# Left factors of the output and FFN projections: turned blocks kept in SBUF, their sums and splits placed by written lists

## The chip, the cores and the metric

One Trainium2 chip, one core. The metric is the device time of one execution in microseconds (us); lower is better. The kernel before takes 1965.07 us, the median of 3 runs (1964.33 to 1965.67). Traces come from one execution each, taken by the hardware profiler.

## What is computed

One layer of a decoder, for 512 tokens (S) of width 2048 (D), all in float32. Cut to what matters here:

```python
h    = rms_norm(x, norm1_g)
proj = h @ w_in                                    # 512 x 2048 @ 2048 x 6160
qa, ka, va, ra, ga, qb, kb, vb = split(proj)
out_a = rms_norm(gated_linear_attention(qa, ka, va, gate(ga))) * silu(ra)   # 4 heads, 512 x 1024
out_b = dilated_attention(norm(qb), norm(kb), vb)                           # 8 heads, 512 x 1024
x  = x + concat(out_a, out_b) @ w_out              # 512 x 2048 @ 2048 x 2048
h2 = rms_norm(x, norm2_g)
x  = x + (silu(h2 @ w_gate) * (h2 @ w_up)) @ w_down   # hidden width 5632
```

## The kernel before

**Products.** Each large matrix product is cut in 2 x 2 blocks and done with seven block products in place of eight (Strassen's way). The left factor of each of the seven is a block of the activations or a sum of blocks; its names are A11, S1, S2, S4, S3, A12 and A22, in the order in which `PRODUCTS` uses them (P1, P5, P6, P3, P7, P2, P4). The right factor is a block of the weights or a difference of blocks. To keep float32 accuracy, each factor is split in a rounded high part and a low remainder, both fp32r, and TensorE multiplies high by high, low by high and high by low: 12 matmuls of 128x512.

**Pairs and items.** A `Pair` (L236) computes 1024 output columns. It is a chain of *items*: seven products times the operand's *groups* (4 as a rule, each 256 + 256 rows of the contraction), so 28 items of 12 matmuls, 336 in all (L358). `stream` (L318) runs all pairs back to back. For item k it emits the high part of the weights of item k+1 (ACT, L331), the difference of weight blocks for item k+2 where the product needs one (DVE, L256; P5, P6, P7 and P4 do), the low part of item k+1 (DVE, L335), then the matmuls of item k. The high and the low weight tiles have two buffers each, so these two engines can be about one item ahead of TensorE.

**The order of the pairs.** Input projection: va, qb0/kb0, vb, qb1/kb1, and the *gate pair* (the columns ra). Output projection: *out0* and *out1*. Then eleven FFN pairs (*ffn0* to *ffn10*), then six down-projection pairs. The left factors of the output projection are held by `opm`, those of the FFN by `opn`.

**Making a left factor.** `Operand.split` (L161, L162) makes one of seven factors of one group: a cast on ACT and a subtraction on DVE, each 128x512. The four sums S1 to S4 take four more DVE operations of that size for each group. So one group costs 11 DVE operations of 128x512, 7 of them the remainders of splits. I call each of these 11 a *unit*.

**Results of a pair.** When a product's last item is done, `later` closes the result some items later: the two row halves of each 512-column half come out after items 15 (P3), 19 (P7), 23 (P2) and, in the next pair, after its item 0 (P4). In the gate pair `final_gate` (L1037) multiplies them by the mixed output of the first heads; in out0 and out1 `final_out` (L1201) adds the residual. Two items after that, `transposed_store` (L1012) turns the 256x512 piece with 8 TensorE transposes (L1019), copies the two 128x512 blocks out of PSUM on ACT (L1027, L1030) and stores each of them in DRAM (L1034): `mix_d` for the gate pair and the dilated heads, `xn_d` for out0 and out1. All DMAs of this part are issued by one queue, SP.

**Background work.** What a later pair needs runs as generators in the list `background`. After the high matmuls of each item `step` (L519) fires what `later` has put off and then takes as many units of the first generator as the pair's pace says. In the gate pair these are the last four dilated heads (`dil_heads(4)`, `dil_heads(6)`), and from `early_job` and `late_jobs` (L1078, L1112) the factors of `opm`: every block is loaded from DRAM again, each time that it is used (`top`, and the tiles r, v, T, qT, kT), 8 loads for each group. `early` (L205) loads two blocks, splits A11, forms S3 (L215) and splits it; `late_jobs` forms S1 (L1121), S2 (L1123), S4 (L1125) with a split each, and splits A12 and A22. Before out0 begins, `finish` (L535) forces `early` to its end, whatever the pace says. For `opn`, groups 0 and 1 are made by `operand_jobs` (L1155, `build` L178) during out1, and groups 2 and 3 by `early_job` and `late_jobs` at the end of out1 and in ffn0, again with `finish` before ffn0.

The order on an engine isn't quite the order in the text: the builder moves an instruction ahead where its inputs are ready, so the text sets priorities and not a fixed sequence. Waits are then met in the order of the engine's queue.

Of the kernel before, what the change touches and what calls it, by code (L numbers as in the profile page):

```python
# [10 lines left out]
F32 = mybir.dt.float32  # L11
# [3 lines left out]
ALU = mybir.AluOpType  # L15
# [3 lines left out]
P = 128  # L19
# [4 lines left out]
DK = 128  # L24
DV = 256
NB = 640
PRODUCTS = ("P1", "P5", "P6", "P3", "P7", "P2", "P4")
UPPER_FIRST = ("P1", "P2", "P5", "P6", "P3", "P7", "P4")

# [67 lines left out]
def block_kernel(ctx: ExitStack, tc: tile.TileContext, ins, out):  # L97
# [19 lines left out]
    def nm(s):  # L117
        uid[0] += 1
        return f"{s}_{uid[0]}"
# [846 lines left out]
    def in_turn(*gens):  # L966
        for g in gens:
            yield from g


    def heads_norm(t):
# [4 lines left out]
        for h in range(4):  # L976
# [35 lines left out]
    def transposed_store(tiles, half, dsts, gains=None, spare=None):  # L1012

        for b in range(2):
            bk = bank().rearrange("p (j n) -> p j n", j=2)
            for jj in range(2):
                for m in range(2):
                    f = (2 * b + jj) * P
                    nc.tensor.transpose(  # L1019
                        bk[:, jj, m * P : (m + 1) * P], tiles[m][:, f : f + P], ident  # L1020
                    )
            if spare is None:
                d = work(("oT", "PT")[b], (P, 2, 256))
            else:
                d = spare[:, b]
            if gains is None:
                nc.scalar.copy(d, bk)  # L1027
            else:
                for jj in range(2):
                    nc.scalar.activation(  # L1030
                        d[:, jj, :], bk[:, jj, :], AF.Copy,
                        scale=gains[:, 2 * b + jj : 2 * b + jj + 1],
                    )
            store(dsts[b][half], d)  # L1034
            done.add((id(dsts[b]), half))

    def final_gate(half, which, tiles, acc_):  # L1037
# [11 lines left out]
        for m in range(2):  # L1049
# [10 lines left out]
            nc.scalar.activation(tiles[m], tiles[m], AF.Ln, bias=1.0)  # L1060
            nc.scalar.activation(tiles[m], tiles[m], AF.Exp, scale=-1.0)
            nc.vector.tensor_tensor(tiles[m], tiles[m], og[m], op=ALU.mult)
        spare = apool.tile([P, 2, 2, 256], F32, name=nm("turned"), tag="A")
        later(2, lambda: transposed_store(
            tiles, half, mix_d[2 * which : 2 * which + 2], spare=spare
        ))

    def part(src, half):
        def get(t=None):
# [4 lines left out]
            return t  # L1074

        return get

    def early_job(op, wanted, flip):  # L1078
        h0, h1 = (1, 0) if flip else (0, 1)
        return op.early([(g, part(top, h0), part(top, h1)) for g, top in wanted])  # L1080

    def staged(items, ahead=1):

# [25 lines left out]

        return (id(src), half), fetch  # L1110

    def late_jobs(op, groups, tops, bots, flip):  # L1112

        h0, h1 = (1, 0) if flip else (0, 1)
        tt = nc.vector.tensor_tensor
        sums = {}

        def sum_of(name, g, op1):
            def use(t):
                if name == "S1":  # L1120
                    tt(sums[g], t, sums[g], op=ALU.add)  # L1121
                elif name == "S2":
                    tt(sums[g], sums[g], t, op=ALU.subtract)  # L1123
                else:
                    tt(sums[g], t, sums[g], op=ALU.subtract)  # L1125
                op.split(name, g, sums[g])

            return use

        def both(g):  # L1130
            fetch = fetch_part(tops[g], h1)[1]

            def get():
                sums[g] = part(bots[g], h1)()
                return fetch()

            return (id(bots[g]), h1), get

        items = []
        for part_ in groups:  # L1140
            for g in part_:
                items.append((*both(g), sum_of("S1", g, op)))
            for g in part_:
                items.append((*fetch_part(tops[g], h0), sum_of("S2", g, op)))
        groups = [g for part_ in groups for g in part_]
        for g in groups:
            items.append((*fetch_part(bots[g], h0), sum_of("S4", g, op)))
        for name, half in (("A12", h0), ("A22", h1)):
            for g in groups:
                items.append(  # L1150
                    (*fetch_part(bots[g], half), lambda t, name=name, g=g: op.split(name, g, t))
                )
        return staged(items)

    def operand_jobs(op, tops, bots, lo, hi):  # L1155
        def job():
# [30 lines left out]
    def residual(tiles, acc_, rows, c0, src):  # L1187
# [10 lines left out]
                res.append(tiles[m])  # L1198
        return res

    def final_out(second):  # L1201
        def final(half, which, tiles, acc_):
            tok = 1 - half
            rows = [2 * tok, 2 * tok + 1]
            ch = 2 * second + which
            tiles = residual(
                tiles, acc_, rows, 512 * ch, lambda t, c: x[t * P : (t + 1) * P, c : c + 512]
            )
            for m in range(2):
                t = rows[m]  # L1210
                store(x1_d[t][:, 512 * ch : 512 * ch + 512], tiles[m])
                jk = work("L", bufs=2)
                nc.scalar.activation(
                    jk, tiles[m], AF.Square, accum_out=ss2[:, t, ch : ch + 1]
                )
            dsts, gains = xn_d[2 * ch : 2 * ch + 2], g2[:, 4 * ch : 4 * ch + 4]

            def turn():
                transposed_store(tiles, tok, dsts, gains)
                if not second and which == 0 and half == 1:  # L1220
                    background.append(operand_jobs(opn, tops, bots, 0, 2))
                elif second and which == 1 and half == 1:
                    background.append(early_job(opn, [(g, tops[g]) for g in (2, 3)], False))
                    background.append(late_jobs(opn, ((2, 3),), tops, bots, False))

            later(3 if which == 0 and half == 1 else 2, turn)
            if second and which == 0 and half == 1:
                for n in range(3):
                    later(1 + n, lambda n=n: output_scales(n))

        return final

    ocol = lambda c: w_out[:, c // 512]
    def output_scales(part):
# [6 lines left out]
        else:  # L1241
# [190 lines left out]
```

## Time and profile before

| | |
|---|---|
| median of 3 runs | 1965.07 us |
| profiled execution | 1958.01 us, span 1956.1 us |
| TensorE's granted clock, mean | 0.999 |
| ACT busy | 1088.1 us, 56% of the span |
| DMA moved | 362.52 MB, 185 GB/s |
| HBM read, written | 298.68 MB, 64.51 MB |

The span runs from the first to the last instruction in the trace; the profiled execution lasted 1.9 us longer than it. In the profile PE is TensorE's matmuls, PEld its weight loads, DVE VectorE, ACT ScalarE, SP the queue that issues the DMAs; L358 is line 358 of the kernel. A window's row gives its length, and for each engine the busy time and, after an x, the number of instructions. A row of a timeline gives start, duration, engine, line, what is written from what, and in brackets how long the engine was idle before it and what ended that. Records of a few matmuls can be missing or stand in a neighbouring window.

### The profile page before, as it was taken

How to read it: one execution, taken by the hardware profiler on the slowest of the kernel's cores; microseconds unless marked ns; L12 is line 12 of the kernel's file. 1: busy time of each engine (PE TensorE's matmuls, PEld its weight loads, DVE VectorE, ACT ScalarE, POOL GpSimd, SP SyncE). 2: the span in 40 equal slices, each digit the busy share in tenths (PEclk: the TensorE clock that was granted, in tenths of full speed). 3: DMA queues.
4: the chain of work that ended last, by engine and by line, in shares of the span. 5: the costliest groups of instructions: out<-in, count | busy, mean ns of one | idle time of the engine just before them, and what ended most of it. 6: DMA issues, size and time to landing. Idle time of an engine off the chain costs nothing.

```text
span 1956.1 us, 25599 instructions
## 1 busy us (share of the span) xinstructions
PE 1918.2 (98%) x9160; PEld 1657.3 (85%) x9160; DVE 1648.0 (84%) x1845; ACT 1088.1 (56%) x1580; POOL 55.2 (3%) x73
## 2 busy tenths in 40 slices
PE   8999999999999999999999999999999999999998
PEld 6788888888878888888888888888888888888887
DVE  7996887768789989878878879879879989989977
ACT  9654554667666665544544545545546646546443
POOL 0000330011000000000000000000000000000000
PEclk9999999999999999999999999999999999999999
DMA  9545555444567584453453453443445865855662
GB/s 355 174 154 206 179 173 171 143 156 162 198 217 241 181 289 148 154 188 141 155 183 135 162 182 120 171 171 124 173 170 176 279 212 182 292 198 180 230 215 76
DMA packets 158855, 362.52 MB, mean 185 GB/s; under 512 B 16438, under 2 KB 43359, under 8 KB 158728
## 3 DMA queue, kind: packets, MB, share of 16 engines
q1 hardware_dynamic: 158584, 360.89, 53.1%
q8 instruction: 71, 1.16, 0.2%
q14 instruction: 56, 0.46, 0.1%
q10 hardware_dynamic: 144, 0.01, 0.0%
HBM read 298.68 MB, written 64.51 MB: 186 GB/s over the span
## 4 chain that ended last, share of the span: by engine, by line
PE 75%; DVE 6%; DMA 3%; issue 2%; ACT 1%; SPq 0%; POOL 0%; DVEq 0%; ACTq 0%
PE acc L358 71%; DVE wl L335 2%; PE bank L1019 1%; DVE wa L256 1%; PE bank L926 1%; PE bank L904 1%; DVE AS L162 1%; PE bank L919 0%; DMA xn_d<-PT 0%; DMA q<-y_d 0%; PE bank L895 0%; DMA q<-in_x 0%; DMA T<-p_d 0%; DMA r<-xn_d 0%; ACT wh L331 0%
## 5 line engine op out<-in xcount | busy, mean ns | idle before, releaser
L358 PE MATMUL acc<-wh,AS 128*128 128x512 f32 x3008 | 712.2, 379 | 0.9 <-DVE AS L162 0.8
L358 PEld LDWEIGHTS acc<-wh,AS 128*128 128x128 f32 x3008 | 568.0, 189 | 82.8 <-DVE AS L162 1.6
L331 ACT CAST wh<-wa 128x1024 fp32r<-128x1024 f32 x376 | 394.3, 1049 | 395.1 <-PE acc L358 365.2
L358 PE MATMUL acc<-wh,AA 128*128 128x512 f32 x2256 | 533.7, 379 | 1.1 <-ACT wh L331 0.9
L335 DVE TENSOR_TENSOR wl<-wa,wh 128x1024 fp32r<-128x1024 f32 x376 | 458.7, 1223 | 74.5 <-ACT wh L331 45.6
L358 PEld LDWEIGHTS acc<-wh,AA 128*128 128x128 f32 x2256 | 426.0, 189 | 62.7 <-ACT wh L331 2.3
L358 PE MATMUL acc<-wl,AS 128*128 128x512 f32 x1504 | 395.3, 385 | 7.6 <-DVE wl L335 7.5
L358 PEld LDWEIGHTS acc<-wl,AS 128*128 128x128 f32 x1504 | 279.2, 189 | 61.0 <-DVE wl L335 20.3
L358 PE MATMUL acc<-wl,AA 128*128 128x512 f32 x1128 | 296.1, 385 | 3.4 <-DVE wl L335 3.3
L358 PEld LDWEIGHTS acc<-wl,AA 128*128 128x128 f32 x1128 | 209.3, 189 | 35.8 <-DVE wl L335 7.5
L331 ACT CAST wh<-wb 128x1024 fp32r<-128x1024 f32 x94 | 98.6, 1049 | 123.8 <-PE acc L358 117.1
L331 ACT CAST wh<-wc 128x1024 fp32r<-128x1024 f32 x94 | 98.4, 1047 | 109.2 <-PE acc L358 106.6
L331 ACT CAST wh<-wd 128x1024 fp32r<-128x1024 f32 x94 | 98.6, 1049 | 103.6 <-PE acc L358 98.5
L335 DVE TENSOR_TENSOR wl<-wc,wh 128x1024 fp32r<-128x1024 f32 x94 | 115.0, 1223 | 41.7 <-ACT wh L331 41.7
L335 DVE TENSOR_TENSOR wl<-wd,wh 128x1024 fp32r<-128x1024 f32 x94 | 114.8, 1223 | 37.8 <-ACT wh L331 28.7
L256 DVE TENSOR_TENSOR wa<-wc,wa 128x1024 f32<-128x1024 f32 x94 | 114.8, 1225 | 35.6 <-DMA wc<-in_w_gate 20.8
L335 DVE TENSOR_TENSOR wl<-wb,wh 128x1024 fp32r<-128x1024 f32 x94 | 114.5, 1221 | 5.3 <-ACT wh L331 4.9
L256 DVE TENSOR_TENSOR wa<-wb,wa 128x1024 f32<-128x1024 f32 x94 | 113.8, 1222 | 1.7 <-DMA wb<-in_w_in 1.0
L256 DVE TENSOR_TENSOR wb<-wd,wb 128x1024 f32<-128x1024 f32 x94 | 114.8, 1223 | 0.4
L256 DVE TENSOR_TENSOR wa<-wd,wa 128x1024 f32<-128x1024 f32 x94 | 113.5, 1223 | 0.1
L298 DVE SCALAR_TENSOR_TENSOR seed<-acc,rs,seed 128x512 f32<-128x512 f32 x96 | 70.5, 747 | 27.6 <-PE acc L358 27.5
L282 ACT ACTIVATE seed<-acc,rs 128x512 f32<-128x512 f32 x96 | 60.8, 682 | 3.1 <-PE acc L358 3.1
(285 smaller groups left out, 1332.2 us busy)
## 6 DMA issues: line engine op xcount, KB each, us to landing
wa<-in_w_gate SPq DMA_DIRECT2D x44, 512.0 KB, 3.4
wb<-in_w_up SPq DMA_DIRECT2D x44, 512.0 KB, 4.0
wd<-in_w_up SPq DMA_DIRECT2D x44, 512.0 KB, 4.1
wc<-in_w_gate SPq DMA_DIRECT2D x44, 512.0 KB, 3.4
wc<-in_w_in SPq DMA_DIRECT2D x28, 512.0 KB, 3.5
wa<-in_w_in SPq DMA_DIRECT2D x24, 512.0 KB, 4.9
wb<-in_w_in SPq DMA_DIRECT2D x24, 512.0 KB, 5.7
wd<-in_w_in SPq DMA_DIRECT2D x24, 512.0 KB, 5.1
```

The source lines that it names most:

```text
L162: nc.vector.tensor_tensor(a[:, :, 1, :], src, a[:, :, 0, :].bitcast(F32), op=ALU.subtract)
L256: nc.vector.tensor_tensor(src, self.quarter(one, g), src, op=ALU.subtract)
L282: nc.scalar.activation(halves(t), unfolded(src[m]), AF.Copy, scale=self.scale(half, m))
L298: nc.vector.scalar_tensor_tensor(halves(seed[m]), unfolded(src[m]), self.scale(half, m), halves(seed[m]), op0=ALU.mult, op1=ALU.add,)
L331: nc.scalar.copy(high[k], sources[k])
L335: nc.vector.tensor_tensor(low[k], sources.pop(k), high[k].bitcast(F32), op=ALU.subtract)
L358: nc.tensor.matmul(p.dst[prod][m], a[:, jj, hl, m * P : (m + 1) * P], folded(w[:, jj, :]), start=fresh and g == 0 and len(terms) == 2 and ...
L904: nc.tensor.matmul(lp[:, :n], qh[:, b * P : (b + 1) * P], kh[:, :n], start=True, stop=True)
L926: nc.tensor.matmul(op, vh[:, k, :], lgs[b][:, k * P : (k + 1) * P], start=(k == 0), stop=(k == b))
L1019: nc.tensor.transpose(bk[:, jj, m * P : (m + 1) * P], tiles[m][:, f : f + P], ident)
```

## The change

The text of the four pairs around the output projection is changed in three ways.

1. **The gate pair's turned blocks stay in SBUF.** `transposed_store` gets no destination there, so the 8 stores to `mix_d` are gone; the blocks lie in tiles of `apool` or in the work tiles qT, kT, v, T, and are found in `kept`. The blocks of the dilated heads still go through DRAM, and each is now loaded once (`T`), kept, and used for A11, S3, S2 and S1. S2 is formed before S1, in place: S2 = r1 - S3, then S1 = S2 + A11.
2. **The same for the second half of `opn`**: out1's turned blocks stay in work tiles ("t") and in `rpool` ("r"), and `kept_job` makes groups 2 and 3 in the order of `KEPT`, without a load or a store.
3. **Where the units stand.** In the gate pair and in out0 a written list says after which item's step each unit is emitted; `early_job`, `late_jobs` and the forced `finish` before out0 are gone. The `finish` before ffn0 now asks for A11 of group 3 only. The paces of ffn0 change, and out0's last result is turned one item earlier.

```diff
+KEPT = "A11.2 A11.3 =S3.2+S3.2 =S3.3+S3.3 =S2.2+=S1.2+S1.2 =S2.3+=S1.3+S1.3 S2.2 S2.3 =S4.2+S4.2 =S4.3+S4.3 A12.2 A12.3 A22.2 A22.3"
+GATE = {
+    9: "T.0 T.1",  11: "A11.0",  12: "S3.0",  13: "A11.1",  14: "S3.1",  16: "T.2",
+    18: "A11.2",  19: "S3.2",  21: "2.0 S1.0",  22: "2.1",  23: "S1.1",  24: "S2.0",
+    25: "T.3 S2.1",  27: "A11.3",
+}
+OUT = {
+    0: "S3.3",  2: "2.2 S1.2",  3: "2.3 S1.3",  4: "S2.2",  5: "S2.3",  9: "S4.0",
+    10: "S4.1",  11: "S4.2",  12: "S4.3",  17: "A12.0 A12.1",  18: "A12.2",  19: "A12.3",
+    21: "A22.0",  22: "A22.1",  24: "A22.2",  25: "A22.3",
+}
...
         "qb1": lambda: [
             dil_heads(4),
-            together(dil_heads(6), in_turn(*(early_job(opm, [(g, mix_d[4 + g])], True) for g in range(3)))),
-            early_job(opm, [(3, mix_d[7])], True),
-            late_jobs(opm, ((0, 1), (2, 3)), mix_d[4:], [mix_d[b] for b in order], True),
+            dil_heads(6),
         ],
...
+            if dsts is None:
+                continue
             store(dsts[b][half], d)
...
-        spare = apool.tile([P, 2, 2, 256], F32, name=nm("turned"), tag="A")
-        later(2, lambda: transposed_store(
-            tiles, half, mix_d[2 * which : 2 * which + 2], spare=spare
-        ))
+        def turn():
+            if which == 1:
+                t = apool.tile([P, 2, 2, 256], F32, name=nm("turned"), tag="A")
+                spare = [t[:, 0], t[:, 1]]
+            else:
+                spare = [work(n, (P, 2, 256)) for n in (("qT", "kT"), ("v", "T"))[half]]
+            transposed_store(tiles, half, None, spare=spare)
+            for b in range(2):
+                kept[2 * (which == 0) + b, "r" + str(1 - half)] = spare[b]
+        later(2, turn)
...
+        if name == "T":
+            t = apool.tile([P, 2, 2, 256], F32, name=nm("top"), tag="A")
+            for i in range(2):
+                kept[g, "t" + str(i)] = part(mix_d[4 + g], 1 - i)(t[:, i])
+            return
+        t0, t1 = kept[g, "t0"], kept[g, "t1"]
+        if name == "A11":
+            opm.split(name, g, t0)
+        elif name == "S3":
+            tt(t1, t0, t1, op=ALU.subtract)
+            opm.split(name, g, t1)
+        elif name == "2":
+            tt(t1, kept[g, "r1"], t1, op=ALU.subtract)
+            tt(t0, t1, t0, op=ALU.add)
+        elif name == "S1":
+            opm.split(name, g, t0)
+        elif name == "S2":
+            opm.split(name, g, t1)
+        elif name == "S4":
+            tt(t1, kept[g, "r0"], t1, op=ALU.subtract)
+            opm.split(name, g, t1)
+        else:
+            opm.split(name, g, kept[g, "r0" if name == "A12" else "r1"])
...
-    pair(opx, rows_in, col(2048), col(2560), final_gate, rate((27, 0.72), (1, 0)), row_scale)
+    pair(opx, rows_in, col(2048), col(2560), final_gate, scripted(rate((27, 0.72), (1, 0)), GATE), row_scale)
...
             def turn():
-                transposed_store(tiles, tok, dsts, gains)
-                if not second and which == 0 and half == 1:
-                    background.append(operand_jobs(opn, tops, bots, 0, 2))
-                elif second and which == 1 and half == 1:
-                    background.append(early_job(opn, [(g, tops[g]) for g in (2, 3)], False))
-                    background.append(late_jobs(opn, ((2, 3),), tops, bots, False))
-
-            later(3 if which == 0 and half == 1 else 2, turn)
+                if not second:
+                    transposed_store(tiles, tok, dsts, gains)
+                    if which == 0 and half == 1:
+                        background.append(operand_jobs(opn, tops, bots, 0, 2))
+                        background.append(kept_job(opn, kept_n))
+                    return
+                if which == 1:
+                    kept_n["t", tok] = [work(n, (P, 2, 256)) for n in (("qT", "kT"), ("v", "T"))[tok]]
+                else:
+                    kept_n["r", tok] = [
+                        rpool.tile([P, 2, 256], F32, name=nm("r"), tag="r") for _ in range(2)
+                    ]
+                transposed_store(tiles, tok, None, gains, spare=kept_n["tr"[which == 0], tok])
+
+            later(2, turn)
...
-    pair(opm, rows_mix, ocol(0), ocol(512), final_out(0), paced([1] * 28),
-         before=lambda: finish(lambda: ("S3", 3) in opm.t))
+    pair(opm, rows_mix, ocol(0), ocol(512), final_out(0), scripted(step, OUT))
...
-    paces = {0: [0, 1, 1, 1, 1, 0, 0, 1, 1] + [0] * 6, 10: [0] * 6}
+    paces = {0: [1, 1, 1, 1, 0, 0, 0, 0, 0, 0, 1, 1, 1, 1, 0, 0, 0, 0], 10: [0] * 6}
     def before_ffn(j):
         if j == 0:
-            finish(lambda: ("S3", 3) in opn.t)
+            finish(lambda: ("A11", 3) in opn.t)
```

The lists are shortened here to fewer lines. `scripted` (not shown) calls the pair's pace and then emits the words that the list has for the item. `kept_job` (not shown) goes through `KEPT`, one word for each step; it waits, without emitting anything, until the blocks that a word needs are there; a word with "=" forms the sum, one without it is the split.

More of the change, by code (lines that the diff above doesn't have):

```diff
@@ L1110, in fetch_part @@
         return (id(src), half), fetch
-    def late_jobs(op, groups, tops, bots, flip):
-        h0, h1 = (1, 0) if flip else (0, 1)
-        tt = nc.vector.tensor_tensor
[L1116 to L1153, printed above, removed]
@@ L1199, in residual, with kept_job @@
         return res
+    kept_n = {}
+    def kept_job(op, kept):
+        tt = nc.vector.tensor_tensor
+        sums = {
+            "S3": ("t1", "t0", "t1", ALU.subtract), "S2": ("t1", "r1", "t1", ALU.subtract),
+            "S1": ("t0", "t1", "t0", ALU.add), "S4": ("t1", "r0", "t1", ALU.subtract),
+        }
+        parts = {"A11": "t0", "S3": "t1", "S1": "t0", "S2": "t1", "A12": "r0", "S4": "t1", "A22": "r1"}
+        have = lambda n: (n[0], int(n[1])) in kept
+        for word in KEPT.split():
+            for one in word.split("+"):
+                name, *g = one.split(".")
+                split = name in parts and one[0] != "="
+                name = name.strip("=")
+                g = int(g[0])
+                needs = [parts[name]] if split else sums[name][:3]
+                while not all(have(n) for n in needs):
+                    yield
+                at = lambda n: kept[n[0], int(n[1])][g - 2]
+                if split:
+                    op.split(name, g, at(parts[name]))
+                else:
+                    d, a, b, how = sums[name]
+                    tt(at(d), at(a), at(b), op=how)
+            yield
     def final_out(second):
```

47 lines of the change are left out of this document (43 added, 4 removed).

## Prediction

> **What bounds the kernel now.** I read the page first.
>
> ```profile
> span 1956.1 us, 25599 instructions
> PE 1918.2 (98%) x9160; PEld 1657.3 (85%) x9160; DVE 1648.0 (84%) x1845; ACT 1088.1 (56%) x1580; POOL 55.2 (3%) x73
> q1 hardware_dynamic: 158584, 360.89, 53.1%
> ```
>
> TensorE bounds the whole, with VectorE close behind as an average. So I looked for stages in which TensorE runs below its pace: windows of the item line alone, cut so that each holds one pair of 336 matmuls (gate pair, out0, out1, ffn0, ffn1), then the same windows for the transposes (L1019; out0, out1, ffn0, ffn1), and from the chain the price of eight transposes.
>
> ```profile
> 453.37:558.54 105.17, 78.64 (x338) 62.45 (x336) 1.00 0.54 187
> 558.54:642.12 83.58, 76.09 (x338) 62.41 (x336) 1.00 0.64 214
> 642.12:720.81 78.69, 75.32 (x337) 62.21 (x336) 1.00 0.64 219
> 720.81:801.98 81.17, 74.49 (x336) 62.97 (x337) 1.00 0.57 193
> 801.98:876.27 74.29, 73.03 (x337) 63.20 (x336) 1.00 0.45 160
> ```
>
> ```profile
> 558.54:642.12 83.58, 5.25 (x38) 4.29 (x38) 1.00 0.64 214
> 642.12:720.81 78.69, 4.15 (x32) 3.75 (x32) 1.00 0.64 219
> 720.81:801.98 81.17, 2.08 (x16) 1.87 (x16) 1.00 0.57 193
> 801.98:876.27 74.29, 2.07 (x16) 1.87 (x16) 1.00 0.45 160
> ```
>
> ```profile
> 809.05 0.87 PE bank L1019 x8
> ```
>
> ffn1 is the undisturbed pair: 74.29 us, with 16 transposes at 0.87/8 = 0.109. Without them (1.74) 336 matmuls take 72.55, so 0.216 each and 2.59 for an item. Above that pair, and with 0.109 for every further transpose taken off, out0 loses 83.58 - 74.29 - 22 x 0.109 = **6.9 us**, out1 78.69 - 74.29 - 16 x 0.109 = **2.7**, ffn0 81.17 - 74.29 = **6.9**. The gate pair carries the dilated heads' matmuls too, so there I take only the visible idle time of PE, from windows of all engines (columns: PE, PEld, DVE, ACT, POOL, clock, DMA share, GB/s):
>
> ```profile
> 453.37:500.00 46.63, 44.76 (x237) 37.44 (x236) 38.22 (x63) 32.34 (x74) 4.88 (x4) 1.00 0.34 111
> 500.00:544.40 44.40, 43.98 (x241) 38.19 (x240) 35.07 (x63) 32.10 (x65) 0.00 (x0) 1.00 0.64 224
> 544.40:558.54 14.14, 13.04 (x65) 10.86 (x63) 9.90 (x14) 9.31 (x14) 0.00 (x0) 1.00 0.91 322
> 558.54:597.99 39.45, 35.09 (x159) 27.69 (x158) 39.42 (x48) 26.46 (x39) 0.00 (x0) 1.00 0.38 127
> 597.99:642.12 44.13, 44.13 (x219) 38.81 (x217) 42.61 (x49) 30.27 (x51) 0.00 (x0) 1.00 0.87 292
> 698.00:720.81 22.81, 22.70 (x113) 19.53 (x112) 16.46 (x19) 13.18 (x25) 0.00 (x0) 1.00 0.96 325
> 720.81:759.66 38.85, 33.43 (x152) 27.67 (x153) 36.56 (x46) 26.59 (x44) 0.00 (x0) 1.00 0.52 174
> 801.98:876.27 74.29, 74.29 (x353) 65.01 (x352) 60.28 (x59) 37.15 (x43) 0.00 (x0) 1.00 0.45 160
> ```
>
> That is 1.87 + 0.42 + 1.10 = **3.4 us**. So everything within reach of this change is 6.9 + 2.7 + 6.9 + 3.4 = 19.9 us, about 1% of the span. The rows also say where it lies: all of out0's loss is in its first 12 items (from 597.99 on PE is busy without a gap), and there DVE is busy 39.42 of 39.45 us. All of ffn0's loss is in its first 12 items too (12 x 2.59 + 0.87 = 32.0 of 38.85), with DVE at 36.56. Just ahead of both, DVE stood still: 4.2 us in 544.40 to 558.54, 6.4 in 698 to 720.81.
>
> The clearest view is the ledger of loads. PEld is busy 65.01/74.29 = 87.5% in the undisturbed pair, 70% in out0's first 12 items and 71% in ffn0's. [...]
>
> What DVE did, and what PE waited for, from their timelines:
>
> ```profile
> 465.65 0.68 DVE L162 TENSOR_TENSOR AA<-top,AA 128x512 fp32r<-128x512 f32 x1
> ...
> 548.31 0.69 DVE L1121 TENSOR_TENSOR r<-v,r 128x512 f32<-128x512 f32 x1 [3.91 <-DMA v<-mix_d]
> ...
> 556.05 0.69 DVE L215 TENSOR_TENSOR top<-top 128x512 f32<-128x512 f32 x1
> ...
> 560.55 1.22 DVE L335 TENSOR_TENSOR wl<-wa,wh 128x1024 fp32r<-128x1024 f32 x1
> ...
> 562.82 0.69 DVE L162 TENSOR_TENSOR AA<-top,AA 128x512 fp32r<-128x512 f32 x1
> 563.42 0.69 DVE L162 TENSOR_TENSOR AS<-top,AS 128x512 fp32r<-128x512 f32 x1
> 564.03 0.69 DVE L162 TENSOR_TENSOR AS<-r,AS 128x512 fp32r<-128x512 f32 x1
> ...
> 596.81 0.68 DVE L1125 TENSOR_TENSOR r<-qT,r 128x512 f32<-128x512 f32 x1
> ...
> 619.62 0.69 DVE L162 TENSOR_TENSOR AA<-kT,AA 128x512 fp32r<-128x512 f32 x1
> ```
>
> ```profile
> 719.25 0.69 DVE L215 TENSOR_TENSOR top<-top 128x512 f32<-128x512 f32 x1 [3.08 <-DMA top<-xn_d]
> 719.86 0.69 DVE L162 TENSOR_TENSOR AA<-top,AA 128x512 fp32r<-128x512 f32 x1
> 722.42 0.69 DVE L215 TENSOR_TENSOR top<-top 128x512 f32<-128x512 f32 x1 [1.87 <-DMA top<-xn_d]
> ...
> 754.22 0.69 DVE L162 TENSOR_TENSOR AS<-r,AS 128x512 fp32r<-128x512 f32 x1
> ```
>
> ```profile
> 559.56 0.88 PE L1019 MATMUL bank<-mats,seed 128*128 128x128 f32 x6 [0.64 <-DVE seed L1062]
> ...
> 577.12 1.13 PE L358 MATMUL acc<-wl,AS 128*128 128x512 f32 x4 [0.88 <-DVE wl L335]
> ```
>
> DVE stands in its queue before a sum whose block is on its way back from DRAM, the weights' low part (wl) stands behind that sum, and PE waits for wl. Units follow each other every (564.03 - 562.82)/2 = 0.605 us though each lasts 0.69. Of opm's 44 units DVE does 12 before out0 begins (465.65 to 556.05), 21 in its first 12 items (562.82 to 596.81) and 11 later (to 619.62). Of opn's 22 for groups 2 and 3 it does 2 before ffn0 (719.25, 719.86), 16 in the first 12 items (722.42 to 754.22), 4 later.
>
> **The change part by part.**
>
> *Removed DMAs.* 16 stores and 40 loads of 256 KB, 14.7 of 362.5 MB. DMA isn't what PE waits for in these stretches except through the sums, so by themselves 0.
>
> *The waits.* DVE's 3.91 at 544.40, and 3.08 + 1.87 around ffn0's start, are waits for blocks that now never leave SBUF. DVE gets that time back.
>
> *DVE's work.* No unit disappears: a group still needs 4 sums and 7 splits. They move. By the lists, before out0's item 0 stand A11 of four groups (4), S3 of three (6), the two sums of groups 0 and 1 (4), S1.0, S1.1, S2.0, S2.1 (4): 18 in place of 12. In items 0 to 11 stand 16 (S3.3, the sums and S1 of groups 2 and 3, S2.2, S2.3, S4.0 to S4.2), in place of 21: 5 x 0.605 = 3.0 us less. The 10 left come later, where PE has no gap to widen so far.
>
> *out0.* DVE's 39.42 become 36.4; PE needs 12 x 2.59 + 14 x 0.109 = 32.6. DVE is still over by 3.8 in this stretch. Today it also enters late: the low part of item 1 begins 560.55 - 558.54 = 2.0 us after item 0, because 3.91 us were stood away. With two buffers that part can begin when item 0 does, takes 1.2, and is needed 2.59 + 8 x 0.216 = 4.3 after it: a cushion of 3.1. A DVE that enters on time spends the cushion on the 3.8. What is left is 0.7 by this sum; as the units come in lumps (three in each of items 2 and 3) I take 1.5. Gain 6.9 - 1.5 = **5.4**; bounds 0 (the moved units only delay the gate pair) and 6.9.
>
> *ffn0.* By `KEPT` and the new paces, 9 units stand in out1 in place of 2, and 10 in ffn0's first 12 items in place of 16: 6 x 0.605 = 3.6 us less, and the 38.85 - 36.56 = 2.3 us of DVE idle in it go: 5.9 of 6.9. The 7 units that out1's end takes are 4.2 us, against 6.4 of DVE idle there. Lumps again (three units in item 0 beside a residual sum): gain **5.2**; bounds 0 and 6.9.
>
> *Gate pair.* The early units move from items 4 to 13 to items 11 to 19, the 6 further units (3.6 us) stand in its last third, where DVE is idle for 4.2 us after 544.40 and for part of the 44.40 - 35.07 = 9.3 before. The last turned block's transposes wait for late multiplications (the 0.64 above is the second such wait); an unblocked DVE ends that: **1.0**, bounds -3 (the moved units push P4's low parts) and 3.4.
>
> *out1* stays: operand_jobs starts an item earlier, the same 14 units, 0 with bounds -1 and 1. ACT's casts and copies are the same in number; ACT is busy 26.46 of 39.45 in the worst stretch, so they stay hidden.
>
> Sum: 5.4 + 5.2 + 1.0 = 11.6 us. The profiled execution took 1958.01, 7.1 below the median of the runs, so I expect 1946.4 for such an execution and 1965.07 - 11.6 = **1953.5** as the median.
>
> **The rivals.**
>
> *Half of it (20%).* DVE's total is unchanged, so the lists only move the shortage. For: 597.99 to 642.12 has DVE at 42.61 of 44.13, 1.5 us free, and 10 units (6.1) come in; an overrun of 4.6 less a cushion of 3.1 gives 1.5 back, and the gate pair may give back 3. Against: before, the 11 late units were in the same window. Then 11.6 - 1.5 - 4 = about 6: 1959.
>
> *More (7%).* The lists leave nearly no gap, out1 included: 17 to 19 us, 1947.
>
> *No change (8%).* Bound by the busiest engine: PE shows 98%, DMA 53%, and the change takes work off DMA alone. Then 1965. [...] The stretches above speak against it here: PE's 98% hides 70%.
>
> *Slower (10%).* A11.3 in the way. The loads of the last head's block are now written at item 25, later than today's:
>
> ```profile
> 541.93 0.38 SPq L942 DMA_DIRECT2D mix_d<-oT x1
> ...
> 548.84 0.97 SPq L1073 DMA_DIRECT2D top<-mix_d x2
> ...
> 554.80 1.69 SPq L222 DMA_DIRECT2D wd<-in_w_out x3
> ```
>
> ```profile
> top<-mix_d SPq DMA_DIRECT2D x8, 256.0 KB, 4.6
> ```
>
> If they queue behind the three weight loads at 554.80 they land at about 554.80 + 1.69 (their issue) + 0.97 (its own issue) + 4.6 (landing) = 562. If the builder also puts A11.3's cast and remainder ahead of the next weights' in ACT's and DVE's queues, wl of item 1 waits from 558 to 563 and the shortage of out0 (3.8) comes on top with no cushion: about 9 lost there against 6.9 today, and with -3 in the gate pair and ffn0's gain gone if out1's DVE is as crowded, 1969. It decides once the block lands after about 559. [...] Against: the first row shows the heads storing their part of that block at 542, so the loads can be hoisted, and A11.3 is needed only 3 items later.
>
> **How the numbers follow.** Forecast (8 to 15 us gained) 55%, half 20%, more 7%, none 8%, slower 10%. A measurement here tells about 0.2% (3.9 us) from no change: faster 82%, same 8%, slower 10%. The range of 80% runs from 1947 (18 gained) to 1962 (3 gained).
>
> **What would show it.** Right: no DVE wait for `mix_d` or `xn_d` sums around 544 and 719; out0 at 78 us, ffn0 at 76; PEld near 84% in their first 12 items; out1 at 78 to 79; DVE's total unchanged. Wrong: gaps of PE before wl in the gate pair's last product or in out0's items 16 to 27, or ACT waiting for `top` at out0's start.

## The result and the profile after

| | before | after |
|---|---|---|
| median of 5 runs | 1965.07 us (1964.33 to 1966.78) | 1954.71 us (1951.73 to 1958.18) |
| ratio, 95% interval | | 0.995 (0.9937 to 0.9963) |
| profiled execution | 1958.01 us | 1957.12 us |

The change gains 10.4 us, where 11.6 were forecast. The two profiled executions differ by only 0.9 us; a repeat of the kernel before (e4, below) shows why they can't be subtracted. The page of the kernel after, its first lines and its DMA queue:

```profile
span 1955.0 us, 25520 instructions
PE 1921.6 (98%) x9160; PEld 1665.2 (85%) x9160; DVE 1647.8 (84%) x1845; ACT 1089.6 (56%) x1580; POOL 48.7 (2%) x73
q1 hardware_dynamic: 150520, 346.21, 53.3%
```

Nothing there tells of a gain: same work on PE and DVE, 14.7 MB less on the queue. The stages do. Windows of the item line alone (now L393) for the gate pair, out0, out1, ffn0 and ffn1, then of the transposes (now L1052) for out0:

```profile
460.71:570.33 109.62, 80.75 (x338) 63.88 (x336) 0.97 0.50 162
570.33:647.94 77.61, 74.29 (x338) 62.96 (x336) 1.00 0.46 158
647.94:724.50 76.56, 73.92 (x337) 62.90 (x336) 1.00 0.64 211
724.50:799.54 75.04, 73.38 (x338) 63.19 (x337) 1.00 0.41 130
799.54:873.83 74.29, 73.03 (x337) 63.20 (x336) 1.00 0.49 161
```

```profile
570.33:647.94 77.61, 4.43 (x32) 3.65 (x32) 1.00 0.46 158
```

Against before, out0 is 83.58 - 77.61 = 6.0 us shorter, out1 2.1, ffn0 6.1, and the gate pair 4.5 **longer**: 9.8 in all. Parts of these stages in windows of all engines: the gate pair's end, out0's first 12 items, the rest of out0, out1's end, ffn0's first 12 items.

```profile
556.19:570.33 14.14, 14.14 (x75) 12.34 (x73) 12.18 (x17) 11.47 (x18) 0.00 (x0) 1.00 0.84 284
570.33:603.87 33.54, 32.94 (x153) 27.68 (x152) 33.54 (x38) 23.49 (x34) 0.00 (x0) 1.00 0.03 10
603.87:647.94 44.07, 44.07 (x218) 38.78 (x216) 43.12 (x50) 30.01 (x50) 0.00 (x0) 1.00 0.80 270
701.69:724.50 22.81, 22.81 (x115) 20.04 (x114) 20.67 (x26) 16.22 (x31) 0.00 (x0) 1.00 0.91 306
724.50:757.12 32.62, 32.22 (x153) 27.96 (x152) 32.62 (x42) 23.95 (x39) 0.00 (x0) 1.00 0.07 28
```

Twelve items that took 39.45 and 38.85 us take 33.54 and 32.62. DVE, still busy throughout both, stands still for 2.1 us in out1's end in place of 6.4. Its timeline there and around out0's start:

```profile
555.77 1.22 DVE L370 TENSOR_TENSOR wl<-wa,wh 128x1024 fp32r<-128x1024 f32 x1 [1.99 <-PE acc L393]
...
570.24 0.68 DVE L197 TENSOR_TENSOR AA<-top,AA 128x512 fp32r<-128x512 f32 x1
...
571.98 1.22 DVE L370 TENSOR_TENSOR wl<-wa,wh 128x1024 fp32r<-128x1024 f32 x1
...
574.44 0.68 DVE L197 TENSOR_TENSOR AS<-top,AS 128x512 fp32r<-128x512 f32 x1
...
603.30 1.28 DVE L197 TENSOR_TENSOR AS<-top,AS 128x512 fp32r<-128x512 f32 x2
```

```profile
713.25 0.69 DVE L329 TENSOR_TENSOR seed<-acc,seed 128x512 f32<-128x512 f32 x1 [1.53 <-PE acc L393]
...
722.07 1.22 DVE L370 TENSOR_TENSOR wl<-wa,wh 128x1024 fp32r<-128x1024 f32 x1
```

No sum waits for DRAM at these two places any more (a new wait, of 1.05 us in the gate pair's item 14, comes up below). Where DVE waits there, it waits for PE: it is ahead. Counting the sums and split remainders in these timelines, 20 of `opm`'s 44 units start before out0 (the last at 570.24), 13 in its first 12 items (574.44 to 603.30), 11 later; the lists name 18, 16 and 10. The builder took two more ahead.

### The profile page after: what moved, and what is told of

It reads as the page before. It is cut to its first block, busy times and chain, and to the rows that moved or that the text cites. A ratio compares the mean times of both kernels' runs of the same rounds, so it can differ in the third digit from the quotient of the medians.

```text
span 1955.0 us, 25520 instructions
## 1 busy us (share of the span) xinstructions
PE 1921.6 (98%) x9160; PEld 1665.2 (85%) x9160; DVE 1647.8 (84%) x1845; ACT 1089.6 (56%) x1580; POOL 48.7 (2%) x73
## 4 chain that ended last, share of the span: by engine, by line
PE 73%; DVE 6%; DMA 3%; issue 2%; ACT 1%; SPq 0%; POOL 0%; DVEq 0%; ACTq 0%; POOLq 0%
PE acc L393 69%; DVE wl L370 3%; PE bank L1052 1%; DVE wa L291 1%; PE bank L961 1%; PE bank L939 1%; DMA wc<-in_w_in 1%; DVE AS L197 1%; DMA q<-y_d 0%; PE bank L954 0%; ACT wh L366 0%; DMA k<-y_d 0%; DVE seed L329 0%; DVE seed L1233 0%; DVE AA L197 0%
## 5 line engine op out<-in xcount | busy, mean ns | idle before, releaser
L393 PE MATMUL acc<-wh,AS 128*128 128x512 f32 x3008 | 713.6, 380 | 0.0
L393 PEld LDWEIGHTS acc<-wh,AS 128*128 128x128 f32 x3008 | 569.4, 189 | 81.1 <-ACT wh L366 0.3
L393 PE MATMUL acc<-wh,AA 128*128 128x512 f32 x2256 | 533.8, 379 | 2.7 <-ACT wh L366 2.6
L393 PEld LDWEIGHTS acc<-wh,AA 128*128 128x128 f32 x2256 | 425.9, 189 | 64.5 <-ACT wh L366 4.1
L393 PE MATMUL acc<-wl,AS 128*128 128x512 f32 x1504 | 394.6, 384 | 3.5 <-DVE wl L370 3.4
L393 PEld LDWEIGHTS acc<-wl,AS 128*128 128x128 f32 x1504 | 280.4, 189 | 53.5 <-DVE wl L370 11.5
L393 PE MATMUL acc<-wl,AA 128*128 128x512 f32 x1128 | 295.5, 384 | 0.7 <-DVE wl L370 0.7
L393 PEld LDWEIGHTS acc<-wl,AA 128*128 128x128 f32 x1128 | 209.6, 189 | 31.6 <-DVE wl L370 2.9
```

Of the source, the lines that this page charges most:

```text
L393: nc.tensor.matmul(p.dst[prod][m], a[:, jj, hl, m * P : (m + 1) * P], folded(w[:, jj, :]), start=fresh and g == 0 and len(terms) == 2 and ...
```

## The experiments

No kernel here leaves a part of the reference out; e11 adds operations and e7 stores that nobody reads. The stages of all profiles, in us. "16+17" are the gate pair's items 16 and 17, "18-27" its end; items are counted from 0. "Start" is where the gate pair begins. The ratio compares with the kernel before, run beside each.

| | start | gate | 16+17 | 18-27 | out0 | out1 | ffn0 | ratio of times, 95% |
|---|---|---|---|---|---|---|---|---|
| before | 453.4 | 105.2 | 6.9 | 38.9 | 83.6 | 78.7 | 81.2 | |
| before, again (e4) | 457.6 | 105.7 | 7.2 | 38.7 | 83.6 | 80.3 | 80.8 | 1.0008 (0.9999, 1.0017) |
| FFN part (e1) | 456.6 | 107.2 | 6.9 | 39.1 | 83.6 | 78.6 | 76.4 | 0.9964 (0.9951, 0.9978) |
| mix part (e2) | 456.4 | 109.3 | 10.3 | 38.1 | 77.6 | 77.5 | 80.5 | 0.996 (0.9947, 0.9973) |
| after | 460.7 | 109.6 | 10.5 | 38.1 | 77.6 | 76.6 | 75.0 | 0.995 (0.9937, 0.9963) |
| after, again (e9) | 455.7 | 107.9 | 10.2 | 38.1 | 77.6 | 76.6 | 75.0 | 0.9954 (0.9942, 0.9967) |
| reload (e5) | 462.3 | 109.0 | 8.2 | 40.0 | 78.3 | 80.0 | 78.2 | 0.9983 (0.9974, 0.9992) |
| dead stores (e7) | 458.4 | 108.6 | 8.4 | 39.1 | 77.6 | 77.6 | 76.0 | 0.9951 (0.9935, 0.9966) |
| old places (e6) | 456.0 | 107.8 | 7.0 | 39.9 | 78.4 | 77.0 | 75.0 | 0.9935 (0.9921, 0.9949) |
| old places, again (e10) | 455.7 | 106.5 | 6.9 | 40.0 | 78.4 | 77.0 | 75.0 | 0.9942 (0.993, 0.9954) |
| eight more units (e11) | 454.7 | 107.7 | 8.3 | 38.1 | 82.1 | 77.9 | 75.2 | 0.9973 (0.996, 0.9987) |
| late T.2 (e3) | 458.1 | 107.4 | 7.8 | 38.4 | 77.4 | 78.2 | 75.0 | 0.9949 (0.9935, 0.9962) |
| T.2 early, splits late (e12) | 457.5 | 109.8 | 10.3 | 38.4 | 77.4 | 77.9 | 75.0 | 0.9948 (0.9936, 0.9961) |
| tuned (e8) | 460.0 | 104.7 | 6.9 | 38.4 | 77.5 | 77.8 | 75.5 | 0.994 (0.9926, 0.9953) |

**The two halves, each alone.** e1 is the kernel before with `KEPT`, `kept_job` and ffn0's new paces for `opn`:

```diff
-                    background.append(early_job(opn, [(g, tops[g]) for g in (2, 3)], False))
-                    background.append(late_jobs(opn, ((2, 3),), tops, bots, False))
+                        background.append(kept_job(opn, kept_n))
...
-            finish(lambda: ("S3", 3) in opn.t)
+            finish(lambda: ("A11", 3) in opn.t)
```

e2 is the kernel before with the kept blocks and the two lists for `opm`:

```diff
-    pair(opm, rows_mix, ocol(0), ocol(512), final_out(0), paced([1] * 28),
-         before=lambda: finish(lambda: ("S3", 3) in opm.t))
+    pair(opx, rows_in, col(2048), col(2560), final_gate, scripted(rate((27, 0.72), (1, 0)), GATE), row_scale)
+    pair(opm, rows_mix, ocol(0), ocol(512), final_out(0), scripted(step, OUT))
```

> The kernel before with the second half of opn alone changed (out1's turned blocks kept, KEPT's order, the new paces of ffn0); gate pair and out0 as before. If the two boundaries are independent: ffn0 falls from 81.2 to about 75 us, out1 by up to 2, gate pair and out0 stay at 105.2 and 83.6; about 7 us less than before (0.35%). Rival, one shortage that only moves (what the later stage gains the earlier one has paid): out1 gets longer by about as much as ffn0 gains, total within 2 us of before.

> The changed kernel with the old text for out1 and ffn0: only the gate pair's blocks are kept and the lists GATE and OUT used. If independent: out0 about 78 us, gate pair about 109.5 (both as in the changed kernel), ffn0 back at 81; total 1.5 to 3 us less than before. Rival: out0's gain depends on nothing behind it but ffn0 also gains, since DVE reaches the end of out0 with less behind it: ffn0 under 79.

The windows of all engines, out0's and ffn0's first 12 items, of e1 and then of e2:

```profile
563.84:603.35 39.51, 35.16 (x160) 27.73 (x159) 39.48 (x48) 26.53 (x39) 0.00 (x0) 1.00 0.41 127
725.99:759.99 34.00, 32.75 (x153) 27.83 (x152) 32.70 (x43) 23.82 (x39) 0.00 (x0) 1.00 0.10 36
```

```profile
565.73:599.27 33.54, 32.92 (x153) 27.68 (x152) 33.54 (x38) 23.49 (x34) 0.00 (x0) 1.00 0.03 10
720.86:759.08 38.22, 34.78 (x153) 28.98 (x153) 36.77 (x46) 26.41 (x44) 0.00 (x0) 0.96 0.52 173
```

Each half repairs its own stretch (e1's to 34.00, where both halves together reach 32.62) and leaves the other as it was, to 0.7 us. The gate pair's loss comes with the mix half. In time, though, each half gains 7 to 8 us, and both together 9 to 10; for e2 only 1.5 to 3 had been expected. By stages e1 gains about 4.5 in ffn0, and e2 6.0 in out0 less some 4 in the gate pair; over the four stages of the table that is 2.8 and 3.6 us against the first profile of before, 4.5 and 5.3 against its repeat. What is left over, 2 to 5 us each, lies outside these four stages, and it stays open. So the stages show where each half works, and not the whole of its gain in time.

**The kernel before once more.** No edit; it asks whether the first profile of before was an ordinary one.

> The kernel before, unchanged, for its mean granted clock and its start in runs of its own. Its first profile had a clock of 0.999 and the first pair done at 97.7 us, the changed kernel's 0.996 and 103.8 us. Theory: the start is slow in most executions of either kernel, so the first profile of before was a lucky one: clock 0.995 to 0.997, first pair done at 103 to 105 us, span about 1962. Rival: the changed kernel starts slower than before: clock 0.999 and 97 to 98 us again, and the 7 us between that profile and the timed runs lie elsewhere.

Its median agrees with the kernel before run beside it (1964.65 and 1963.4). Its four stages agree with the first profile to 0.5 us in three and 1.6 in out1, but its span is 1962.6 and the gate pair starts 4.2 us later. Over all 14 profiles that start lies between 453.4 and 462.3, and the first profile of before is the earliest of them. The kernel after began its gate pair at 460.7 in its profile, 7.3 us later than before, which hides most of the 9.8 us gained by stages. So the whole spans of two profiles can't be subtracted here; the stages around the change can. What I had expected of its clock did not come: 0.999 in both profiles.

**The round trip put back.** e5 keeps every place and tile of after, but stores each turned block and loads it again; `kept_n` is treated likewise with `xn_d`. e7 has the stores of e5 without the loads.

```diff
-            transposed_store(tiles, half, None, spare=spare)
+            transposed_store(tiles, half, mix_d[2 * which : 2 * which + 2], spare=spare)
+            for b in range(2):
+                load(spare[b], mix_d[2 * which + b][half])
```

> The changed kernel, but each turned block is stored to DRAM and loaded back into its own tile before it is used (16 stores and 16 loads of 256 KB more; lists and order of the text unchanged). Theory W (the gain comes from the waits for the way through DRAM): out0 returns to 81 to 84 us, ffn0 to 78 to 81, about 6 to 8 us slower than the changed kernel. Theory P (the gain comes from the places in the lists, and the round trip is hidden where the lists leave two or more items for it): out0 stays at 77 to 79, and only ffn0 loses, where A11 of groups 2 and 3 stands in the same step as the turned block: 77 to 79; 2 to 4 us slower than the changed kernel.

> The changed kernel with the 16 stores of turned blocks to DRAM put back, though nobody reads them (4.2 MB more written). If DMA work by itself costs nothing here, within 1 us of the changed kernel, each stage within its spread. Rival (DMA is near full in 610 to 650 and 700 to 720, so weights come late): gate pair to ffn0 2 us or more longer.

In time e7 can't be told from after (1955.31 beside 1954.71). Its stages can: the gate pair's end takes 39.1 us, out1 77.6 and ffn0 76.0, each 1 us above after and e9, which agree with each other to 0.1 there. out1 is as long in e3, e11 and e12, which have no such stores, but for the other two the cause shows in DVE's rows of e7:

```profile
560.35 1.31 DVE L1091 TENSOR_TENSOR og<-seed,og 128x512 f32<-128x512 f32 x2 [0.85 <-DMA og<-ong_d]
...
723.61 0.69 DVE L1228 TENSOR_TENSOR q<-acc,q 128x512 f32<-128x512 f32 x1 [0.88 <-DMA q<-in_x]
```

Neither operation waits in after. The first load stands behind two stores in SP's queue and is issued 1.5 us later, counted from the pair's end, than in after; the second is issued at the same distance as in after, while the DMA share in out1's end reads 1.02 in place of 0.91. So the stores cost about 1 us at each place, and the rival of e7 (2 us or more) is not excluded.

e5 loses two thirds of the gain in time, as its theory W had it, but its out0 stays at 78.3, as theory P had it. Windows of e5: out0's first 12 items, out1's end, ffn0's first 12; then DVE's and PE's rows at out1's end:

```profile
571.22:605.45 34.23, 32.96 (x153) 27.75 (x152) 34.23 (x40) 22.73 (x33) 0.00 (x0) 1.00 0.22 74
706.50:729.56 23.06, 20.44 (x103) 17.45 (x101) 14.54 (x18) 11.46 (x21) 0.00 (x0) 1.00 0.91 304
729.56:765.45 35.89, 34.82 (x153) 29.01 (x154) 35.89 (x46) 26.40 (x44) 0.00 (x0) 0.95 0.36 127
```

```profile
727.96 0.69 DVE L1263 TENSOR_TENSOR v<-qT,v 128x512 f32<-128x512 f32 x1 [3.85 <-DMA qT<-xn_d]
```

```profile
729.56 3.08 PE L393 MATMUL acc<-wh,AA 128*128 128x512 f32 x8 [2.62 <-ACT wh L366]
```

The round trip costs where the next use is close: in out1's last items DVE stands 3.85 us, PE then 2.62, and ffn0 starts behind, at a clock of 0.95. out0 hardly notices (34.23 beside 33.54); its lists leave items between a block and its first sum, which is the likely reason. The gate pair's end loses 1.9 us (40.0 beside 38.1), of which the stores alone cost 1.0 in e7.

**The old places.** e6 and e10 are one kernel: blocks kept in SBUF as in after, but the units of `opm` in about the order of before. The lists from item 16 of `GATE` and in `OUT` (S4, A12 and A22 follow there, one word for each item from 8 to 19):

```diff
-    16: "T.2", 18: "A11.2", 19: "S3.2", 21: "2.0 S1.0", 22: "2.1", 23: "S1.1", 24: "S2.0",
-    25: "T.3 S2.1", 27: "A11.3",
+    19: "T.2", 21: "A11.2", 22: "S3.2", 25: "T.3", 26: "A11.3", 27: "S3.3",
...
-    0: "S3.3",  2: "2.2 S1.2",  3: "2.3 S1.3",  4: "S2.2",  5: "S2.3",  9: "S4.0",
+    0: "2.0 S1.0",  1: "2.1 S1.1",  2: "S2.0",  3: "S2.1",  4: "2.2 S1.2",  5: "2.3 S1.3",
+    6: "S2.2",  7: "S2.3",  8: "S4.0",
```

> The changed kernel with the blocks kept in SBUF, but the words placed as the old text had them: one unit for each item of out0 from item 0 (S1, S2, S4, A12, A22, done after item 19), A11 and S3 alone in the gate pair. Theory W: out0 stays near 78, since no sum waits for DRAM. Theory P: out0 goes back to 81 to 83 us, since 21 or more units stand in its first 12 items again; the gate pair is then at 105 to 107.

> Blocks kept in SBUF, words where the old text had them, a second time and beside the changed kernel: if the lists are worth nothing once the blocks stay in SBUF, within 2 us of the changed kernel, out0 at 78.4 with 16 units in its first 12 items. If the lists are worth what the prediction gave them (3.0 us in out0), slower than the changed kernel by 2 to 3.

Windows of e10: items 16 and 17, the gate pair's end, out0's first 12 items.

```profile
515.34:522.22 6.88, 6.46 (x32) 5.34 (x31) 6.82 (x22) 3.99 (x12) 0.00 (x0) 1.00 0.47 149
522.22:562.20 39.98, 38.19 (x212) 33.00 (x211) 32.86 (x54) 32.22 (x62) 0.00 (x0) 1.00 0.67 222
562.20:596.23 34.03, 33.17 (x154) 27.59 (x152) 34.00 (x40) 23.15 (x34) 0.00 (x0) 1.00 0.00 1
```

out0's stretch is 34.03, within 0.5 of after, though the text asks for 24 units there in place of 16: the builder moved them up by itself (17 before out0, 16 in the stretch), since their inputs were there. So for out0 either is enough, early places with the round trip (e5) or blocks in SBUF with late places; before had neither. Both runs keep a third part of the change, though: the dilated heads' blocks are loaded once and kept. No run puts their repeated loads back alone. In time the old places are at no disadvantage: 1951.71 and 1952.08 in e6 and e10, 1954.71 and 1954.32 in after and e9, with intervals that overlap. They beat the kernel before for certain, and after by a margin that isn't shown. Whatever the lists are worth, it is below 2 or 3 us; the kept blocks, turned ones and heads' ones together, carry the rest.

**Eight more units.** Unread additions of a unit's size, in the stretch that DVE fills:

```diff
-    3: "2.3 S1.3", 4: "S2.2", 5: "S2.3",
+    3: "2.3 S1.3 X.2 X.2", 4: "S2.2 X.2 X.2", 5: "S2.3 X.2 X.2", 6: "X.2 X.2",
```

> The changed kernel with eight more DVE operations of 128x512 in out0's items 3 to 6, whose results nobody reads. If DVE's time in the first 12 items is the bound, each costs its full 0.6 us: out0 4 to 5 us longer, about 82, and the kernel too. Rival (only waits for DRAM ever cost out0 anything; DVE's busy row is full because it works ahead): out0 stays under 79.

Out0's first 12 items in e11:

```profile
562.47:600.51 38.04, 33.47 (x153) 27.52 (x152) 38.04 (x47) 23.07 (x33) 0.00 (x0) 1.00 0.02 9
```

38.04 - 33.54 = 4.5 us for eight, 0.56 each, and 3.4 us in the median (1957.75 beside 1954.32). So DVE alone sets the length of this stretch, and after has no slack left in it.

**The gate pair's loss.** e3 loads group 2's block after item 19 in place of 16 and moves its units with it:

```diff
-    16: "T.2", 18: "A11.2", 19: "S3.2", 22: "2.1", 23: "S1.1",
+    19: "T.2", 22: "2.1 A11.2", 23: "S1.1 S3.2",
```

e12 leaves the load and moves only the units:

```diff
-    18: "A11.2", 19: "S3.2", 22: "2.1", 23: "S1.1",
+    22: "2.1 A11.2", 23: "S1.1 S3.2",
```

e8 is e3 with the items of three units in out0 thinned out:

```diff
-    2: "2.2 S1.2",  3: "2.3 S1.3",
+    1: "2.2 S1.2",  2: "2.3",  3: "S1.3",
```

e9 is the kernel after once more, beside e10, e11 and e12.

> The changed kernel with three words of GATE later: T.2 after item 19 in place of 16, A11.2 after 22 in place of 18, S3.2 after 23 in place of 19. Theory: the gate pair's loss in item 17 (7.9 us for one item) comes from these loads and units standing ahead of the last heads' scores in the queues of SP and DVE; then the gate pair falls from 109.6 to about 106, out0 stays near 78, and the kernel is about 3.5 us faster than the changed one. Rival: the loss is the plain price of doing six units more before out0; then gate pair plus out0 stay at 187 us whatever their order, total within 1 us of the changed kernel.

> The changed kernel with the split of A11.2 and S3.2 later (after items 22, 23) but T.2's loads left after item 16. If the loads in SP's queue ahead of the weights cause the gate pair's loss, items 16 and 17 stay at 10 us or more; if it is the units on DVE ahead of the scores, they fall to 7 to 8, as with all three words later.

> The changed kernel with T.2, A11.2 and S3.2 later in GATE (after items 19, 22, 23) and the lumps in OUT pulled apart (2.2 and S1.2 after item 1, 2.3 after item 2, S1.3 after item 3; the rest as it was). Theory: gate items 16 and 17 take about 7.8 us together in place of 10.5, and out0 loses under 1 us in place of 1.5 in its items 2 to 7: about 77; in all 3 to 4 us less than the changed kernel. Rival: units that leave one item press on the next, out0 stays at 77.6.

> The changed kernel again, beside the next three on one chip: for the spread of its stages. Items 16 and 17 of the gate pair together 10.3 to 10.7 us, out0 77.6, ffn0 75 to 76, whatever the start of the run does (the first weight loads, 98 to 104 us in the profiles so far).

The gate pair's items 16 and 17 and its end, before and after, then SP's, DVE's and PE's rows of after:

```profile
512.76:519.64 6.88, 6.46 (x31) 5.34 (x30) 6.82 (x22) 3.98 (x12) 0.00 (x0) 1.00 0.40 149
519.64:558.54 38.90, 37.80 (x206) 32.31 (x204) 29.02 (x48) 29.66 (x58) 0.00 (x0) 1.00 0.79 275
```

```profile
521.72:532.23 10.51, 8.14 (x31) 6.52 (x30) 9.42 (x24) 4.05 (x12) 0.00 (x0) 0.84 0.52 174
532.23:570.33 38.10, 38.10 (x212) 33.07 (x210) 31.41 (x52) 32.03 (x62) 0.00 (x0) 1.00 0.61 199
```

```profile
513.00 0.79 SPq L1115 DMA_DIRECT2D top<-mix_d  x2
513.84 0.90 SPq L1077 DMA_DIRECT2D og<-ong_d  x2
514.78 5.32 SPq L257 DMA_DIRECT2D wc<-in_w_in  x2
```

```profile
515.63 1.23 DVE L291 TENSOR_TENSOR wa<-wc,wa 128x1024 f32<-128x1024 f32 x1 [2.24 <-DMA wc<-in_w_in]
517.91 0.69 DVE L1176 TENSOR_TENSOR top<-top 128x512 f32<-128x512 f32 x1 [1.05 <-DMA top<-mix_d]
...
524.29 0.28 DVE L942 CUSTOM_DVE_ANT_0 L<-bank,T 128x128 f32<-128x128 f32 x1
```

```profile
527.06 0.30 PE L954 MATMUL bank<-mats,L 128*128 128x128 f32 x1 [2.37 <-DVE L L949]
```

Group 2's block and two more loads stand in SP's queue ahead of two weight loads. DVE waits for a weight, then for the block (1.05) in front of more weight work, so the heads' scores (L942) come late, and PE stands 2.37 us for their transposes; the window shows a clock of 0.84 besides, on which more below. e9 repeats the loss (10.2). In e3 the same wait of PE is 1.36 us and the two items take 7.8; in e8, also with late loads, they take 6.9 as before. e12 with the early load stays at 10.3, so moving the splits does not mend it. The builder put the S3 sum early in e12 too, so whether the load itself or that first sum weighs more stays open. e8's out0 stays at 77.5, as its rival said, so thinning the lumps is worth nothing that shows. In time e3, e12 and e8 can't be told from after: some 3 us are at stake, and the intervals reach 2.5 us to either side.

## Why the prediction was right, step by step

*What bounds the kernel: right.* The windows at 70% of PEld were the place; they now show 27.68/33.54 = 83% and 27.96/32.62 = 86% (84% forecast). My rival "no change", for which the busiest engine bounds the kernel (PE at 98%), would have left them.

*Removed DMAs, 0: too small.* With the stores alone put back (e7) the medians show nothing, but the gate pair's end and ffn0 lose about 1 us each. For the loads 0 holds only where nothing waits for them (e5).

*The waits: gone as forecast, but one was misread.* At the two places no sum waits for DRAM. The 3.08 and 1.87 us before ffn0 were for turned blocks, as the prediction says. The 3.91 us at 544.40 were not: the block in tile v is that of a dilated head, which still goes through DRAM after the change, and whose stores had been issued by 388.48. Rows of before, PE's and SP's:

```profile
540.26 1.05 PE L926 MATMUL bank<-L,v 128*128 128x128 f32 x8
```

```profile
543.59 0.50 SPq L1107 DMA_DIRECT2D v<-mix_d  x1
```

The last head still read the work tile v until 541.31, and only then was the block loaded into it again, while the loads beside it in the text (T, qT, kT) had been issued from 532.34 to 533.29. The change ends this wait because it loads each head's block once, into a tile of its own. So e5, which puts back the round trip of the turned blocks alone, could not bring this wait back.

*out0, 5.4 with 1.5 left: right in size; the mechanism failed in part.* 77.61 - 74.29 - 16 x 0.109 = 1.6 us are left, so 5.3 gained (the other 0.7 of the 6.0 are transposes that moved out). But I had DVE entering on time, with a cushion of 3.1. The low part of item 1 starts at 571.98, 1.65 us after item 0 and not with it; before it was 2.0. So an earlier entry is hardly what helped: DVE's recovered wait went into two more hoisted units, and the stretch holds 13, not 16: eight fewer, 4.8 us of the 5.9 by which DVE's time there shrank. e11 confirms a unit's price, 0.56 us for the 0.605 counted.

*ffn0, 5.2: 6.1 measured, by another way.* I put 9 units in out1 and 10 in ffn0's first 12 items; there are 6 and 15, against 2 and 16 before. The step that failed is the emission order of `KEPT` read as the order on DVE. What carries the gain is the term that I had at 2.3, the waits, and it is larger: DVE enters ahead by more than the idle time in the stretch. Before, the low part of item 0 began 2.2 us behind the item's start:

```profile
723.03 1.22 DVE L335 TENSOR_TENSOR wl<-wa,wh 128x1024 fp32r<-128x1024 f32 x1
```

After it begins at 722.07, 2.4 us ahead of 724.50. That is 4.65 us earlier, about the 4.2 that DVE no longer idles in out1's end. e5, which differs by the round trip alone, gives 3.2 of the 6.1 us back; about 0.05 x 35.89 = 1.8 of these are the lower clock behind PE's stand of 2.62. What the order of `KEPT` and the new paces add by themselves was not run.

*Gate pair, a gain of 1.0: 4.5 lost; the end alone came out as forecast.* The end, items 18 to 27, where I argued, gained 38.90 - 38.10 = 0.8. That an unblocked DVE is what did it isn't shown: in e7 no sum waits there either, and the end takes 39.1 with the stores alone put back. Items 16 and 17 lost 10.51 - 6.88 = 3.6, beyond my bound of 3 and by another cause than the one I named: not P4's low parts, but group 2's early load in SP's queue ahead of the weights, with the sum that waits for it. I had followed that queue for the last block (the rival "slower", which did not come) and not for group 2's. The remaining 1.6 of the 4.5 lie in items 0 to 15, which take 59.4 to 61.3 us whichever the kernel, for the reason shown last.

*out1, 0: 2.1 gained in the profile,* beyond its bound of 1. Over all profiles it runs from 76.6 to 80.3, and for before alone from 78.7 to 80.3, so its size is loose.

*The sum.* 11.6 forecast, 9.8 by stages, 10.4 in the medians. The gate pair falls 5.5 short of its term, and out1, ffn0 and out0 make up 2.1 + 0.9 + 0.6 of it, so that the sum comes out close is in part luck. The step from a profile to a median failed: I expected 1946.4 for a profiled execution, and it took 1957.12, because I carried over that the first profile of before lay 7.1 us below its median. e4 shows that this was largely its early start: 4.2 of the 6.5 us between the two spans of before.

## What to carry to other kernels

Look for stretches in which the weight loads' share falls (here 70 and 71% beside 87.5%), and ask there which engine enters late and what it waited for just before: a wait that costs nothing where it stands may be paid items later (before, DVE stood 6.4 us in out1's end, where PE stood 0.11, and ffn0's first 12 items lost 6.9). Where a builder reorders by readiness, what makes an operation early is its data being there, and the tile that it writes being free, not its place in a list; count the units in the trace and not in the text. When a load is moved, follow its queue for every one of them, and compare stages around the change rather than spans.

## What the runs showed of the hardware

PE's stand in item 17 cost more than its 2.37 us. Windows of PE alone in the kernel after (length, PE busy, granted clock, DMA share, GB/s), first there, then in the gate pair's item 4, where PE had stood 1.90 us for loads that the change doesn't touch:

```profile
524.00:527.00 3.00, 0.69 (x4) 1.00 0.49 164
527.00:528.00 1.00, 0.94 (x6) 0.96 0.75 242
528.00:529.00 1.00, 1.00 (x4) 0.50 0.64 254
529.00:530.00 1.00, 1.00 (x4) 0.50 0.17 20
530.00:531.00 1.00, 1.00 (x4) 0.50 0.83 279
531.00:532.00 1.00, 1.00 (x5) 0.83 0.56 225
```

```profile
476.00:477.00 1.00, 1.00 (x8) 0.86 0.10 24
477.00:478.00 1.00, 0.85 (x4) 0.50 0.00 0
...
480.00:481.00 1.00, 1.00 (x7) 0.93 0.00 0
```

After this stand the granted clock is 0.50 for 0.04/0.5 + 3 + 0.17/0.5 = 3.4 us, which costs 1.7 more. From 150 us on, the clock stayed at 1.00 behind stands of PE of 1.36 us (e3), 1.49, 1.50, 1.54 and 1.79 (before) and 1.88 (e10), and 0.50 followed stands of 1.81 (e1), 1.90 and 2.37 (after) and 2.62 (e5). In the start, before 150 us, length alone does not decide either: half clock followed a stand of 1.45 us in e5, and none followed one of 2.37 in e11. In the gate pair half clock sorts the table. Items 16 and 17 take 10.2 to 10.5 us in the four runs whose stand there (2.03 to 2.37) brought half clock, and 8.2 to 8.4 in e5, e7 and e11, whose stands of 1.72 to 1.92 did not: the early load costs about 1.5 us as a wait, and 2 more once the clock drops. Items 0 to 15 take 59.4 to 59.8 us in the five profiles without half clock in item 4 (both of before, e8, e9, e10) and 60.8 to 61.3 in the nine with it, on stands of 1.54 to 1.88 and of 1.81 to 1.98 us. So two stands of the same 1.87 us, in e9 and e12, are followed by 59.7 and 61.1 us for these items.

On DVE a ready operation stood behind a waiting one. In the profile before, the remainder AS<-top had its input from ACT at 546.74 + 0.63 = 547.37; DVE stood 3.91 us, until 548.31, for the sum that waited for v, and began the remainder at 550.71:

```profile
546.74 0.63 ACT L161 CAST AS<-top 128x512 fp32r<-128x512 f32 x1
```

```profile
550.71 0.68 DVE L162 TENSOR_TENSOR AS<-top,AS 128x512 fp32r<-128x512 f32 x1
```
